# Small query blocks of attention handled for both heads at once, and the head gains loaded and turned earlier, in a decoder trunk on one core

## The chip, the cores and the metric

The kernel runs on one core of a Trainium2 chip. The metric is the device time of one execution in microseconds (us). TensorE is called PE here, VectorE DVE, ScalarE ACT, GpSimd POOL and SyncE SP; PEld is PE's weight load, which runs beside PE's products.

## What is computed

The reference is a causal trunk over 512 tokens of width 1024: one attention layer, one gated short convolution, and a gated MLP with a depthwise convolution behind each. The attention layer is the part that matters here. Its 16 heads of 64 are split into 8 forgetting heads (softmax with a decay added to the logits) and 8 stick-breaking heads. Cut to that:

```
xn = rms_norm(h, norm_g);  proj = xn @ w_in          # q, k, v and 8 forget logits
q_fox, k_fox = rms_norm(q[:8], fox_q_g), rms_norm(k[:8], fox_k_g)
q_sb,  k_sb  = rms_norm(q[8:], sb_q_g),  rms_norm(k[8:], sb_k_g)
# forgetting heads, a block of 128 queries
logits = q @ k.T * scale + cum_f[q] - cum_f[k];  p = softmax(causal(logits));  o = p @ v
# stick-breaking heads
z = q @ k.T * scale;  log_beta = log_sigmoid(z)
log_one_minus = where(strict, log_sigmoid(-z), 0)
later = reverse_cumsum(log_one_minus) - log_one_minus
w = where(strict, exp(log_beta + later), 0);  o = w @ v
h = h + concat(o_fox, o_sb) @ w_out
```

The four head gains (`fox_q_g` and so on) have 64 numbers each.

## The kernel before

Every float32 product is made of three PE products: each operand is split into a high part `hi` (a rounded copy, made by ACT) and the rest `lo` (a subtraction, made by DVE), and `hi*hi`, `lo*hi` and `hi*lo` are added up in one bank of PSUM. The helper lines are L245 to L247 (weights times the normed activations) and L489 to L491 (the value projection). Weight tiles come by SP's queue as `raw` and are split into `whi` (L227) and `wlo` (L228). PSUM is divided into two banks "a" (accumulators), four banks "b" (logits) and two banks "c" (everything that is turned, and small sums).

**Start.** `x` comes in four pieces by SP's queue (L93). PE warms up (L696) and turns `x` into bank tiles (`take`, L717). ACT and DVE split the turned tiles into `hs_hi` and `hs_lo` (`halves_of`, L721 and L722), and PE runs the first projections between the takes. In this stage `in_line` ties each engine's operations into the written order. ACT's queue carries one load here, `first` (L85), ahead of the function table and a warm-up activation. POOL's queue carries the four loads of the head gains (`load_heads`, L90). The gains become a column per head group in `load_head_gains`: a PE transpose of a 4x128 tile (L151), a DVE copy out (L152) and two DVE scalings (L154). That call is put off by the constant `HEADS` of a planner clock, so it comes out behind the second projection. The evictions of the q and k projections (L579, L575 and L576) multiply by these columns.

**Attention.** The heads go in pairs p = 0 to 7 (0 to 3 forgetting, 4 to 7 stick-breaking), each with query blocks b = 0 to 3; block b sees n = 128(b+1) keys. `logits(p, b)` makes the logits of both heads e = 0, 1 in two "b" banks and then the weights `w`. A forgetting head takes a maximum (L611), an exponential with its sum (L613, ACT), a reciprocal (L615) and a product (L616). A stick-breaking head takes two sigmoids (L620 and L621, ACT), a zero in the last column (L623, POOL), a reverse scan (L625) and a product (L626). `turn(p, b)` turns the weights on PE (L645), one "c" bank per head, and splits them into the high `pt` (L648, ACT) and the low `pt` (L649, DVE). `weigh(p, half)` multiplies by the values (L664 and L665) for two blocks together, and its result leaves through L674, L675 and the split at L330 and L331.

**What sets the order.** A planner clock in the Python code (`spend`, `after`, `fill`) deals out the work: between logits, turn and weigh it pulls products from `fillers`, which are generators of q and k projections (`queries_keys`), value projections (`values`) and half of the output projection (`output(0)`). Sums, norms and row scales of the q and k tiles (L525, L533, L561, each in a "c" bank) are put off by constants. A scheduler underneath orders the instructions of each engine again by their dependences and bank releases, so a change in one place can move others.

After the attention (from about 280 us on) come the second half of the output projection, the MLP, the short convolution and the second MLP; the change touches no line of these.

Of the kernel before, what the change touches and what calls it, by code (L numbers as in the profile page):

```python
# [17 lines left out]
F32 = mybir.dt.float32  # L18
F32R = mybir.dt.float32r
BF16 = mybir.dt.bfloat16  # L20
I32 = mybir.dt.int32
AF = mybir.ActivationFunctionType
ALU = mybir.AluOpType
AX = mybir.AxisListType

P = 128
S = 512
NB = S // P
# [4 lines left out]
HD = 64  # L33
# [4 lines left out]
PT = 2  # L38
WB = 4
PRE = 12.0  # L40
SUM_STEP = 0.6
WARM = 34
HEADS, NORM0 = 4.0, 4.6
ORDER = (1, 0, 1, 1, 1, 1, 3)
SUMS, FLAT, ROWS = 3.0, 1.5, 5.0
NSUMS, NROWS = 4.0, 3.0
# [4 lines left out]
def trunk(  # L51
# [6 lines left out]
    nc = tc.nc  # L58
    act, dve, pe, pool = nc.scalar, nc.vector, nc.tensor, nc.gpsimd
# [4 lines left out]
    tiny = ctx.enter_context(tc.tile_pool(name="tiny", bufs=4))  # L64
# [4 lines left out]
    def bank(tag):  # L69
        n_ps[0] += 1  # L70
        return ps.tile([P, S], F32, tag=tag, name=f"ps{tag}{n_ps[0]}", bufs={"a": 2, "b": 4, "c": 2}[tag])

    def f32(ap):
        return ap.bitcast(F32)
# [11 lines left out]
    heads_in = xin.tile([4, P], F32, tag="heads_in", name="heads_in")  # L86

    def load_heads():
        for i, g in enumerate((fox_q_gain, fox_k_gain, sb_q_gain, sb_k_gain)):
            nc.gpsimd.dma_start(heads_in[i:i + 1, :].rearrange("o (j d) -> o j d", j=2), g[:, None, :].to_broadcast([1, 2, HD]))  # L90

    def load_x(q):
        nc.sync.dma_start(x_tok[:, :, q * 256:(q + 1) * 256], xr[:, :, q * 256:(q + 1) * 256])  # L93

    load_x(0)
    warm = tiny.tile([P, 1], F32, tag="warm", name="warm", bufs=1)
    act.activation(warm, blank[:, 0:1], AF.Copy)

# [18 lines left out]
    ident = const.tile([P, P], F32, tag="ident", name="ident")  # L117
    make_identity(nc, ident)

    begin = const.tile([P, S], BF16, tag="begin", name="begin")  # L120
# [28 lines left out]
    def load_head_gains():  # L149
        t = bank("c")  # L150
        pe.transpose(t[:, 0:4], heads_in, ident[0:4, 0:4])  # L151
        dve.tensor_copy(head_gains, t[:, 0:4])  # L152
        for i in (0, 2):
            dve.tensor_scalar(head_gains[:, i:i + 1], head_gains[:, i:i + 1], HD ** -0.5, None, op0=ALU.mult)  # L154
# [29 lines left out]
    def after(us, fn):  # L184
        later.append((clock[0] + us, len(later), fn))
        later.sort(key=lambda e: e[0])
# [312 lines left out]
    halves, q_scale, done = {}, {}, set()  # L499
# [6 lines left out]
    def queries_keys(p):  # L506
# [73 lines left out]
            sqs.append(sq)  # L580
        after(SUMS, sums)

    def logits(p, b):

        fox = p < 4
        need(("qk", p))
        need("decay")
        (k_hi, k_lo), (q_hi, q_lo) = (halves[p][i] for i in range(2))
        n = (b + 1) * P
        wide = max(n, 256)  # L590
        tok = slice(b * P, n)
        ss = [bank("b") for _ in range(2)]
        for step, (ql, kl) in enumerate(((q_hi, k_hi), (q_hi, k_lo), (q_lo, k_hi))):
            for e in range(2):
                rows = slice(e * HD, (e + 1) * HD)
                pe.matmul(ss[e][:, 0:wide], ql[rows, tok], kl[rows, 0:wide], start=step == 0, stop=not fox and step == 2)  # L596
        if fox:
            for e in range(2):
                rows = slice(e * HD, (e + 1) * HD)
                pe.matmul(ss[e][:, 0:wide], dl[rows, p, tok], dr[rows, 0:wide], start=False, stop=False)  # L600
            for e in range(2):
                pe.matmul(ss[e][:, tok], ident16, mask, start=False, stop=True)
        spend((4 if fox else 3) * wide * 0.00044 + (0.12 if fox else 0))
        ws = []
        for e in range(2):
            s = ss[e]
            w = aw.tile([P, S], F32, tag="w", name=f"w{p}{b}{e}", bufs=WB)
            ws.append(w)
            if fox:
                top = tiny.tile([P, 1], F32, tag="top", name=f"top{p}{b}{e}")  # L610
                dve.reduce_max(top, s[:, 0:n], axis=AX.X, negate=True)  # L611
                total = tiny.tile([P, 1], F32, tag="total", name=f"total{p}{b}{e}")
                act.activation(w[:, 0:n], s[:, 0:n], AF.Exp, bias=top, accum_out=total)  # L613
                inv = tiny.tile([P, 1], F32, tag="inv", name=f"inv{p}{b}{e}")
                dve.reciprocal(inv, total)  # L615
                dve.tensor_scalar(w[:, 0:n], w[:, 0:n], inv, None, op0=ALU.mult)  # L616
            else:
                scale = q_scale[p]
                rest = aw.tile([P, S], F32, tag="rest", name=f"rest{p}{b}{e}")
                act.activation(rest[:, 0:n], s[:, 0:n], AF.Sigmoid, scale=scale[:, 1, b, e:e + 1])  # L620
                act.activation(w[:, 0:n - 1], s[:, 0:n - 1], AF.Sigmoid, scale=scale[:, 0, b, e:e + 1])  # L621

                pool.memset(w[:, n - 1:n], 0.0)  # L623
                back = rest[:, 1:n][:, ::-1]
                dve.tensor_tensor_scan(back, back, begin[:, S - n + 1:S][:, ::-1], 0.0, op0=ALU.mult, op1=ALU.max)  # L625
                dve.tensor_tensor(w[:, 0:n - 1], w[:, 0:n - 1], rest[:, 1:n], op=ALU.mult)  # L626
        return ws

    pts = {}

    def turn(p, b, ws):

        half, n = b // 2, (b + 1) * P
        if b % 2 == 0:
            pts[p, half] = []
            for e in range(2):
                both = [aw.tile([P, NB, 256], F32R, tag=f"pt{i}", name=f"pt{p}{half}{e}{i}", bufs=PT) for i in range(2)]
                for t in both:
                    pool.memset(f32(t[:, 2 * half + 1, 0:P]), 0.0)
                pts[p, half].append(both)  # L640
        at_ = slice((b % 2) * P, (b % 2 + 1) * P)
        for e in range(2):
            t = bank("c")
            for k in range(b + 1):
                pe.transpose(t[:, k * P:(k + 1) * P], ws[e][:, k * P:(k + 1) * P], ident)  # L645
            src = t[:, 0:n].rearrange("p (k q) -> p k q", q=P)
            hi, lo = pts[p, half][e]
            act.activation(hi[:, 0:b + 1, at_], src, AF.Copy)  # L648
            dve.tensor_tensor(lo[:, 0:b + 1, at_], src, f32(hi[:, 0:b + 1, at_]), op=ALU.subtract)  # L649
        spend(0.22 * (b + 1))  # L650

    def weigh(p, half):


        need(("v", p // 2))
        v = v_tiles[p // 2]
        acc = bank("a")
        to = slice(half * 256, (half + 1) * 256)
        last = 2 * half + 1
        for e in range(2):  # L660
            hi, lo = pts[p, half][e]
            for k in range(last + 1):
                w = v[:, k, 2 * (p % 2) + e].rearrange("p i d -> p (i d)")
                pe.matmul(acc[:, e * 256:(e + 1) * 256], w, hi[:, k, :], start=k == 0, stop=False)  # L664
                pe.matmul(acc[:, e * 256:(e + 1) * 256], w, lo[:, k, :], start=False, stop=k == last)  # L665
        spend(0.44 * (last + 1))
        if p == 4 and half == 0:
            o_tiles[1] = mixed(1)
        o_hi, o_lo = o_tiles[p // 4]
        total = work.tile([P, S], F32, tag="y", name=f"o{p}{half}")[:, 0:256]  # L670
        for e in range(2):
            own, other = (slice(i * HD, (i + 1) * HD) for i in (e, 1 - e))
            cols = slice(e * 256, (e + 1) * 256)
            act.activation(total[own, :], acc[other, cols], AF.Copy)  # L674
            dve.tensor_tensor(total[own, :], acc[own, cols], total[own, :], op=ALU.add)  # L675
        split(o_hi[:, p % 4, to], o_lo[:, p % 4, to], total)
# [17 lines left out]
    t = bank("c")  # L694
# [4 lines left out]
    t = bank("c")  # L699
# [24 lines left out]
    def keep(f):  # L724
        t = taken.pop(f)
        if f % 2:
            in_line("act", act.activation(h[:, f, :], t, AF.Copy))
        else:
            in_line("dve", dve.tensor_copy(h[:, f, :], t))
# [7 lines left out]
        load_x(q)  # L737
    for i in range(1, 1 + AHEAD):
        ready.append(load(i))
    load_heads()  # L740
    after(HEADS, load_head_gains)
    qk0 = queries_keys(0)
    part, nk = halve.pop(0)

# [15 lines left out]
    for f in range(2, ND):  # L760
        take(f)
        halves_of(f)
        if f == 3:
            keep(0)
            keep(1)
        first_products(ORDER[f - 1])
# [13 lines left out]
    attn = ExitStack()  # L780
    ap_ = attn.enter_context(tc.tile_pool(name="attn", bufs=1))
    aw = attn.enter_context(tc.tile_pool(name="aw", bufs=2))

# [17 lines left out]
    for g in range(len(blocks) + 2):  # L803
# [3 lines left out]
        if g >= 2 and blocks[g - 2][1] % 2:  # L807
            p, b = blocks[g - 2]
# [41 lines left out]
    with tc.tile_pool(name="mlp0", bufs=1) as mp:  # L850
# [3 lines left out]
        for o in range(ND):  # L854
            acc = bank("ab"[o % 2])
            k = 0
            for nk in (8, 7, 7):
                w = weights()
# [7 lines left out]
    with tc.tile_pool(name="mix", bufs=1) as mp:  # L866
# [23 lines left out]
        for o in range(ND):  # L890
            w = weights()
# [7 lines left out]
    with tc.tile_pool(name="mlp1", bufs=1) as mp:  # L899
        a_hi, a_lo = mlp_tiles(mp)  # L900
        up(1, norm, a_hi, a_lo)
        for c in range(2):
# [16 lines left out]
            for k in range(k0):  # L919
                if k % 2 == 0:  # L920
                    w = weights()
# [4 lines left out]
            ws = [weights(AHEAD - i) for i in range(AHEAD + 1)]  # L926
# [31 lines left out]
```

## Time and profile before

| | |
|---|---|
| median of 3 runs | 1225.56 us |
| range of the runs | 1225.53 to 1226.32 us |
| the profiled execution | 1226.17 us |
| its span in the trace | 1224.4 us |
| PE busy | 1207.0 us, 99% of the span |
| DVE busy | 762.8 us, 62% |
| ACT busy | 502.3 us, 41% |

The span is the stretch that the trace covers; 1.77 us of the profiled execution lie around it. Busy time is an average over the whole program, so the stages have to be looked at one by one. A wait that the trace names is an idle stretch of an engine together with what released it. "idle before" in a row is the time in which the engine did nothing just before that instruction.

### The profile page before, as it was taken

To read this page: it belongs to the slowest core of one execution; us is meant where nothing else is said; L and a number is where in the kernel's file an instruction comes from. 1 tells how busy PE (TensorE), PEld (TensorE's weight loads), DVE (VectorE), ACT (ScalarE), POOL (GpSimd) and SP (SyncE) were. 2 spreads that over 40 slices of the span, in tenths; PEclk is the share of its full clock that TensorE was granted. 3 is DMA by queue.
4 is the path that set the end of the run, shared out by engine and by line. 5 is a ranking of instruction groups with operands and counts; after the bars stand their busy time and mean duration, and the time that the engine had idled before them with its cause. 6 is when DMAs were issued, how large, how long until landed. Compare 5 with 4: busy or idle time off the path is not lost.

```text
span 1224.4 us, 15001 instructions
## 1 busy us (share of the span) xinstructions
PE 1207.0 (99%) x5841; PEld 974.7 (80%) x5841; DVE 762.8 (62%) x1249; ACT 502.3 (41%) x787; POOL 26.5 (2%) x139
## 2 busy tenths in 40 slices
PE   8999999999999999999999999999999999999998
PEld 7887877777888888888888888888888888888886
DVE  5887888887767776763333655555776767772222
ACT  6556576555443434342222222233444444342120
POOL 4000000000000000000000000000000000000000
PEclk9999999999999999999999999999999999999999
DMA  7312121212333333333333233333333233322330
GB/s 195 88 36 69 36 69 36 73 56 80 93 97 91 98 90 100 89 91 95 95 95 103 86 92 97 97 93 92 98 86 103 86 104 86 103 86 86 118 106 35
DMA packets 183576, 108.14 MB, mean 88 GB/s; under 512 B 4716, under 2 KB 176796, under 8 KB 183504
## 3 DMA queue, kind: packets, MB, share of 16 engines
q1 hardware_dynamic: 183104, 107.00, 29.6%
q8 instruction: 46, 0.75, 0.3%
q0 software_dynamic: 384, 0.17, 0.1%
q14 instruction: 26, 0.21, 0.1%
q10 hardware_dynamic: 16, 0.00, 0.0%
HBM read 105.06 MB, written 2.10 MB: 88 GB/s over the span
## 4 chain that ended last, share of the span: by engine, by line
PE 90%; DVE 6%; ACT 2%; issue 1%; POOL 0%; DVEq 0%; ACTq 0%
PE psa L245 13%; PE psa L247 13%; PE psa L246 13%; PE psb L245 11%; PE psb L247 11%; PE psb L246 11%; PE psa L489 2%; PE psa L490 2%; PE psa L491 2%; PE psb L490 2%; PE psb L489 2%; PE psb L491 2%; DVE rest L625 1%; PE psc L645 1%; PE psb L596 1%
## 5 line engine op out<-in xcount | busy, mean ns | idle before, releaser
L227 ACT ACTIVATE whi<-raw 128x1024 fp32r<-128x1024 f32 (+3 forms) x199 | 208.6, 1049 | 361.0 <-PE psb L246 131.1
L228 DVE TENSOR_TENSOR wlo<-raw,whi 128x1024 fp32r<-128x1024 f32 (+3 forms) x199 | 240.5, 1209 | 161.0 <-ACT whi L227 160.0
L245 PE MATMUL psa<-hs_hi,whi 128*128 128x512 f32 x544 | 219.4, 403 | 2.3 <-DVE o L675 1.3
L247 PE MATMUL psa<-hs_hi,wlo 128*128 128x512 f32 x544 | 215.1, 395 | 0.3 <-DVE wlo L228 0.2
L246 PE MATMUL psa<-hs_lo,whi 128*128 128x512 f32 x544 | 214.7, 395 | 0.0
L245 PE MATMUL psb<-hs_hi,whi 128*128 128x512 f32 x480 | 189.9, 396 | 0.0
L247 PE MATMUL psb<-hs_hi,wlo 128*128 128x512 f32 x480 | 189.8, 395 | 0.0
L246 PE MATMUL psb<-hs_lo,whi 128*128 128x512 f32 x480 | 188.8, 393 | 0.0
L338 DVE SCALAR_TENSOR_TENSOR u<-y,taps,u 128x510 f32<-128x510 f32 (+1 forms) x176 | 131.1, 748 | 3.0
L245 PEld LDWEIGHTS psa<-hs_hi,whi 128*128 128x128 f32 x544 | 102.3, 188 | 25.6 <-issue 2.3
L247 PEld LDWEIGHTS psa<-hs_hi,wlo 128*128 128x128 f32 x544 | 102.2, 188 | 25.0 <-DVE wlo L228 1.1
L246 PEld LDWEIGHTS psa<-hs_lo,whi 128*128 128x128 f32 x544 | 102.3, 188 | 22.3 <-DVE hs_lo L722 0.4
L246 PEld LDWEIGHTS psb<-hs_lo,whi 128*128 128x128 f32 x480 | 90.1, 188 | 21.4
L247 PEld LDWEIGHTS psb<-hs_hi,wlo 128*128 128x128 f32 x480 | 90.1, 188 | 21.4
L245 PEld LDWEIGHTS psb<-hs_hi,whi 128*128 128x128 f32 x480 | 90.3, 188 | 20.3
L832 DVE TENSOR_TENSOR y<-psb,nrow_n 128x512 f32<-128x512 f32 x44 | 30.4, 692 | 83.9 <-PE psb L247 83.9
L330 ACT ACTIVATE a<-u 128x512 fp32r<-128x512 f32 x44 | 27.9, 634 | 118.6 <-DVE u L837 118.6
L836 ACT ACTIVATE u<-u 128x512 f32<-128x512 f32 x44 | 27.8, 632 | 91.4 <-DVE u L338 91.4
L335 ACT ACTIVATE u<-y,taps 128x512 f32<-128x512 f32 x88 | 63.0, 719 | 0.0
L331 DVE TENSOR_TENSOR a<-u,a 128x512 fp32r<-128x512 f32 x44 | 30.5, 692 | 29.4 <-ACT a L330 29.4
L489 PE MATMUL psa<-whi,hs_hi 128*128 128x256 f32 (+1 forms) x128 | 38.3, 299 | 0.8 <-ACT qk L579 0.7
L491 PE MATMUL psa<-whi,hs_lo 128*128 128x256 f32 (+1 forms) x128 | 36.3, 283 | 0.0
(237 smaller groups left out, 1824.0 us busy)
## 6 DMA issues: line engine op xcount, KB each, us to landing
raw<-in_ffn_w_up SPq DMA_DIRECT2D x88, 512.0 KB, 3.8
raw<-in_ffn_w_down SPq DMA_DIRECT2D x30, 512.0 KB, 3.6
raw<-in_attn_w_in SPq DMA_DIRECT2D x24, 512.0 KB, 4.0
raw<-in_conv_w_in SPq DMA_DIRECT2D x24, 512.0 KB, 3.8
raw<-in_ffn_w_down SPq DMA_DIRECT2D x16, 448.0 KB, 3.6
raw<-in_attn_w_out SPq DMA_DIRECT2D x8, 512.0 KB, 3.4
raw<-in_conv_w_out SPq DMA_DIRECT2D x8, 512.0 KB, 3.8
x_tok<-in_x SPq DMA_DIRECT2D x4, 512.0 KB, 6.8
```

Of the source, the lines that this page charges most:

```text
L227: return (act.activation(hi[:, at_], raw[:, at_], AF.Copy), dve.tensor_tensor(lo[:, at_], raw[:, at_], f32(hi[:, at_]), op=ALU.subtract))
L228: dve.tensor_tensor(lo[:, at_], raw[:, at_], f32(hi[:, at_]), op=ALU.subtract))
L245: made = [pe.matmul(acc, w[0], rhs[0], start=first, stop=False), pe.matmul(acc, w[0], rhs[1], start=False, stop=False), pe.matmul(acc, w[1 ...
L246: pe.matmul(acc, w[0], rhs[1], start=False, stop=False),
L247: pe.matmul(acc, w[1], rhs[0], start=False, stop=last)]
L331: dve.tensor_tensor(lo, src, f32(hi), op=ALU.subtract)
L335: act.activation(dst, src, AF.Copy, scale=tap(2))
L338: dve.scalar_tensor_tensor(dst[:, d:], src[:, 0:S - d], tap(j), dst[:, d:], op0=ALU.mult, op1=ALU.add)
L489: pe.matmul(acc, lhs[0], w[0], start=first, stop=False)
L490: pe.matmul(acc, lhs[0], w[1], start=False, stop=False)
L491: pe.matmul(acc, lhs[1], w[0], start=False, stop=last)
L832: dve.tensor_tensor(y, acc, norm.row, op=ALU.mult)
```

## The change

1. **Head gains.** The four loads of `load_heads` go to ACT's queue, right behind `first`, and so ahead of ACT's table load. `load_head_gains` is no longer put off: it is called after the fourth take in the start, and the constant `HEADS` goes.
2. **Small blocks.** For b < 2 `at_once` gives one slice with both heads, for b of 2 and 3 two slices with one head. Per slice there is one reciprocal (forgetting) or one product (stick-breaking), one "c" bank for the turned weights, one high copy and one low subtraction. With one slice all of it holds both heads: 2 x 128 or 2 x 256 columns.
3. **Zeros.** `rest` becomes one tile that is kept for the whole attention, with a column of zeros at its end, and a stick-breaking block lies at its right end. The product is taken one column further along and meets the zero, so POOL's memset of the last column of `w` goes. The scan and the second sigmoid are one column longer.
4. **Tiles.** `w` is one tile for both heads (two buffers), and `pt` one tile for both heads (one buffer), so its zeros take half as many memsets, each for both heads.

```diff
-HEADS, NORM0 = 4.0, 4.6
+NORM0 = 4.6
...
-            nc.gpsimd.dma_start(heads_in[i:i + 1, :].rearrange("o (j d) -> o j d", j=2), g[:, None, :].to_broadcast([1, 2, HD]))
+            act.dma_start(heads_in[i:i + 1, :].rearrange("o (j d) -> o j d", j=2), g[:, None, :].to_broadcast([1, 2, HD]))
...
     load_x(0)
+    load_heads()
     warm = tiny.tile([P, 1], F32, tag="warm", name="warm", bufs=1)
...
+    def at_once(b):
+        return (slice(0, 2),) if b < 2 else (slice(0, 1), slice(1, 2))
...
+            for es in at_once(b):
+                dve.reciprocal(inv[:, es], total[:, es])
+                for e in range(es.start, es.stop):
+                    dve.tensor_scalar(w[:, e, :], w[:, e, :], inv[:, e:e + 1], None, op0=ALU.mult)
...
+            for es in at_once(b):
+                for e in range(es.start, es.stop):
+                    act.activation(rest[:, e, keys], ss[e][:, 0:n], AF.Sigmoid, scale=scale[:, 1, b, e:e + 1])
+                    act.activation(w[:, e, :], ss[e][:, 0:n], AF.Sigmoid, scale=scale[:, 0, b, e:e + 1])
+                    back = rest[:, e, keys][:, ::-1]
+                    dve.tensor_tensor_scan(back, back, begin[:, keys][:, ::-1], 0.0, op0=ALU.mult, op1=ALU.max)
+                dve.tensor_tensor(w[:, es], w[:, es], rest[:, es, S - n + 1:S + 1], op=ALU.mult)
...
-        for e in range(2):
-            t = bank("c")
-            for k in range(b + 1):
-                pe.transpose(t[:, k * P:(k + 1) * P], ws[e][:, k * P:(k + 1) * P], ident)
...
+        for es in at_once(b):
+            t = bank("c")[:, 0:(es.stop - es.start) * n].rearrange("p (e k q) -> p e k q", k=b + 1, q=P)
+            for e in range(es.start, es.stop):
+                for k in range(b + 1):
+                    pe.transpose(t[:, e - es.start, k, :], w[:, e, k * P:(k + 1) * P], ident)
+            act.activation(hi[:, es], t, AF.Copy)
+            dve.tensor_tensor(lo[:, es], t, f32(hi[:, es]), op=ALU.subtract)
...
-    load_heads()
-    after(HEADS, load_head_gains)
...
         if f == 3:
+            load_head_gains()
             keep(0)
             keep(1)
...
+    rest = aw.tile([P, 2, S + 1], F32, tag="rest", name="rest", bufs=1)
+    pool.memset(rest[:, :, S:S + 1], 0.0)
```

Lines of the changed kernel are shifted by one in most places (its L246 is L245 of before, its L646 is L645). The change moves instructions in three places that matter here.

PE at the start, before: `first` and the first two takes of `x`, then the first projection.

```order
69 L700 MATMUL psc_150<-ident,first 128x8
70 L717 MATMUL psb_174<-ident,x_tok 128x128 x4
71 L717 MATMUL psb_179<-ident,x_tok 128x128 x4
72 L245 MATMUL psa_194<-hs_hi,whi_155 128x512
73 L246 MATMUL psa_194<-hs_lo,whi_155 128x512
```

The same place of the changed kernel.

```order
69 L699 MATMUL psc_154<-ident,first 128x8
70 L716 MATMUL psb_174<-ident,x_tok 128x128 x4
71 L716 MATMUL psb_179<-ident,x_tok 128x128 x4
72 L152 MATMUL psc_212<-ident,heads_in 128x4
73 L246 MATMUL psa_194<-hs_hi,whi_159 128x512
74 L247 MATMUL psa_194<-hs_lo,whi_159 128x512
```

The transpose of the head gains (`heads_in`) now stands ahead of the first projection, and with it PE's wait for the four loads.

PE behind the second projection, before: L151 turns the head gains, L525 makes the sums of squares, L489 to L491 begin the values (`psa_416` is the accumulator of the first group of 24 products).

```order
125 L247 MATMUL psa_280<-hs_hi,wlo_163 128x512
126 L151 MATMUL psc_260<-ident,heads_in 128x4
127 L525 MATMUL psc_451<-sq_276,head_ones 32x128 x4
128 L489 MATMUL psa_416<-whi_166,hs_hi 128x264
129 L490 MATMUL psa_416<-wlo_167,hs_hi 128x264
```

The same place of the changed kernel; `psa_418` is the first group and `psa_446` the second.

```order
126 L248 MATMUL psa_280<-hs_hi,wlo_167 128x512
127 L490 MATMUL psa_418<-whi_170,hs_hi 128x264
128 L491 MATMUL psa_418<-wlo_171,hs_hi 128x264
...
150 L492 MATMUL psa_418<-whi_282,hs_lo 128x264
151 L526 MATMUL psc_453<-sq_276,head_ones 32x128 x4
152 L526 MATMUL psc_453<-sq_399,head_ones 32x128 x3
153 L490 MATMUL psa_446<-whi_170,hs_hi 128x264
```

The values now follow the projection directly, and the sums stand behind their first group.

PE in block b = 1 of pair 3, before: L645 turns the weights of the two heads into two "c" banks (`psc_2091`, `psc_2096`), and L561 turns the row scales of pair 4 into the next one (`psc_2107`).

```order
869 L645 MATMUL psc_2091<-ident,w_1921 128x128 x2
870 L645 MATMUL psc_2096<-ident,w_1929 128x128 x2
871 L489 MATMUL psa_2087<-whi_1607,hs_hi 128x256
...
886 L489 MATMUL psa_2087<-whi_1751,hs_hi 128x256
887 L561 MATMUL psc_2107<-ident,qwide_2005 128x128 x4
888 L490 MATMUL psa_2087<-wlo_1752,hs_hi 128x256
```

The same place of the changed kernel, where L646 is the turn and L562 the row scales.

```order
864 L646 MATMUL psc_1976<-ident,w_1822 128x128 x4
865 L490 MATMUL psa_1972<-whi_1528,hs_hi 128x256
...
870 L492 MATMUL psa_1972<-whi_1528,hs_lo 128x256
871 L562 MATMUL psc_1989<-ident,qwide_1901 128x128 x4
872 L490 MATMUL psa_1972<-whi_1528,hs_hi 128x256
```

Both heads now share one bank, and the row scales stand 6 products behind the turn, where there were 16.

## Rows read from the trace of the kernel before

**Rows 1.** The page, busy time: us (share of the span), instructions.

```profile
PE 1207.0 (99%) x5841; PEld 974.7 (80%) x5841; DVE 762.8 (62%) x1249; ACT 502.3 (41%) x787; POOL 26.5 (2%) x139
```

**Rows 2.** Windows: length, busy PE, PEld, DVE, ACT, POOL, PE clock, DMA share, GB/s.

```profile
7.00:22.00 15.00, 14.71 (x72) 11.03 (x72) 11.05 (x15) 12.86 (x22) 5.96 (x16) 1.00 0.69 191
50.00:280.00 230.00, 219.66 (x1466) 175.24 (x1465) 186.76 (x465) 140.70 (x321) 13.71 (x92) 0.99 0.19 54
267.00:276.00 9.00, 7.02 (x35) 5.68 (x34) 6.55 (x12) 3.97 (x8) 0.00 (x0) 0.81 0.14 40
280.00:1224.40 944.40, 940.53 (x4081) 760.27 (x4079) 541.91 (x698) 331.58 (x419) 0.00 (x0) 1.00 0.31 93
```

**Rows 3.** Waits of PE, 50 to 280 us: total, times, longest.

```profile
PE psc L645 <- DVE pt L649: 3.6, 4, 1.4
...
PE psc L561 <- DVE pt L649: 1.4, 2, 0.9
...
PE psc L561 <- DVE qwide L554: 0.5, 1, 0.5
```

**Rows 4.** Timeline of PE behind the second projection: start, duration, instruction.

```profile
22.13 0.22 PE L151 MATMUL psc<-ident,heads_in 4*128 4x4 f32 x1
22.86 0.42 PE L525 MATMUL psc<-sq,head_ones 128*32 128x128 f32 x8 [0.51 <-DVE head_gains L152]
23.71 0.39 PE L489 MATMUL psa<-whi,hs_hi 128*128 128x264 f32 x1 [0.42 <-ACT qk L579]
...
27.55 0.43 PE L525 MATMUL psc<-sq,head_ones 128*32 128x128 f32 x8
27.90 0.39 PE L489 MATMUL psa<-whi,hs_hi 128*128 128x264 f32 x1
```

**Rows 5.** Timeline of ACT there.

```profile
24.49 0.72 ACT L579 ACTIVATE qk<-psa,head_gains 128x512 f32<-128x512 f32 x1
```

**Rows 6.** Timeline of PE at the start.

```profile
4.91 1.10 PE L717 MATMUL psb<-ident,x_tok 128*128 128x128 f32 x8
6.99 0.50 PE L245 MATMUL psa<-hs_hi,whi 128*128 128x512 f32 x1 [0.99 <-ACT whi L227]
```

**Rows 7.** Timeline of ACT at the start.

```profile
0.73 0.62 ACTq L85 DMA_DIRECT2D first<-in_attn_norm  x1
...
5.60 0.69 ACT L721 ACTIVATE hs_hi<-psb,first_gains 128x512 fp32r<-128x512 f32 x1 [2.73 <-PE psb L717]
```

**Rows 8.** Timeline of SP's queue at the start.

```profile
1.76 2.67 SPq L93 DMA_DIRECT2D x_tok<-in_x  x3
```

**Rows 9.** DMA queues, 0 to 3.2 us: ACT's queue, which carries `first` alone.

```profile
q10 hardware_dynamic: 16, 0.00, 0.6%
```

**Rows 10.** Line L90, the four loads of the head gains on POOL.

```profile
DMA to landing us min/median/max: 5.0/5.6/5.8
```

**Rows 11.** Timeline of PE in block 1 of pair 3.

```profile
143.40 0.60 PE L645 MATMUL psc<-ident,w 128*128 128x128 f32 x4
...
146.80 0.66 PE L561 MATMUL psc<-ident,qwide 128*128 128x128 f32 x4 [0.92 <-DVE pt L649]
```

**Rows 12.** Timeline of DVE there.

```profile
143.60 0.42 DVE L554 COPY qwide<-qr 128x512 f32<-128x512 f32 x1
...
146.33 0.75 DVE L649 TENSOR_TENSOR pt<-psc,pt 128x256 fp32r<-128x256 f32 x2
```

**Rows 13.** Timeline of PE in block 1 of pair 7.

```profile
256.05 0.47 PE L245 MATMUL psa<-o_hi,whi 128*128 128x512 f32 x1 [0.27 <-DVE o L675]
```

**Rows 14.** DVE groups by shape, 50 to 280 us: busy, mean ns, idle before.

```profile
L615 DVE RECIPROCAL inv<-total 128x1 f32<-128x1 f32 x32 | 5.0, 159 | 2.4 <-ACT w L613 2.4
...
L649 DVE TENSOR_TENSOR pt<-psc,pt 128x128 fp32r<-128x128 f32 x16 | 4.4, 288 | 3.7 <-ACT pt L648 1.6 <-POOL pt L639 1.3 <-POOL w L623 0.8
```

**Rows 15.** Timeline of DVE and PE in block 0 of pair 0, all engines.

```profile
54.00 0.28 DVE L616 TENSOR_SCALAR w<-w,inv 128x128 f32<-128x128 f32 x1
...
55.41 0.27 PE L645 MATMUL psc<-ident,w 128*128 128x128 f32 x1
```

More of the change, by code (lines that the diff above doesn't have):

```diff
@@ L603, in logits @@
         spend((4 if fox else 3) * wide * 0.00044 + (0.12 if fox else 0))
-        ws = []
-        for e in range(2):
[L606 to L626, printed above, removed]
@@ L627, in logits @@
-        return ws
+        w = aw.tile([P, 2, S], F32, tag="w", name=f"w{p}{b}", bufs=2)[:, :, 0:n]
+        if fox:
+            top, total, inv = (tiny.tile([P, 2], F32, tag=t, name=f"{t}{p}{b}") for t in ("top", "total", "inv"))
+            for e in range(2):
+                dve.reduce_max(top[:, e:e + 1], ss[e][:, 0:n], axis=AX.X, negate=True)
+                act.activation(w[:, e, :], ss[e][:, 0:n], AF.Exp, bias=top[:, e:e + 1], accum_out=total[:, e:e + 1])
+            for es in at_once(b):
+                dve.reciprocal(inv[:, es], total[:, es])
+                for e in range(es.start, es.stop):
+                    dve.tensor_scalar(w[:, e, :], w[:, e, :], inv[:, e:e + 1], None, op0=ALU.mult)
+        else:
+            scale = q_scale[p]
+            keys = slice(S - n, S)
+            for es in at_once(b):
[5 more added lines that the diff above has]
+                dve.tensor_tensor(w[:, es], w[:, es], rest[:, es, S - n + 1:S + 1], op=ALU.mult)
@@ L629, in trunk, with turn @@
+        return w
     pts = {}
-    def turn(p, b, ws):
+    def turn(p, b, w):
         half, n = b // 2, (b + 1) * P
         if b % 2 == 0:
[L635 to L642, printed above, removed]
-            t = bank("c")
-            for k in range(b + 1):
-                pe.transpose(t[:, k * P:(k + 1) * P], ws[e][:, k * P:(k + 1) * P], ident)
[L646 to L649, printed above, removed]
+            pts[p, half] = [aw.tile([P, 2, NB, 256], F32R, tag=f"pt{i}", name=f"pt{p}{half}{i}", bufs=1) for i in range(2)]
+            for t in pts[p, half]:
+                pool.memset(f32(t[:, :, 2 * half + 1, 0:P]), 0.0)
+        hi, lo = (t[:, :, 0:b + 1, (b % 2) * P:(b % 2 + 1) * P] for t in pts[p, half])
+        for es in at_once(b):
[5 more added lines that the diff above has]
+            dve.tensor_tensor(lo[:, es], t, f32(hi[:, es]), op=ALU.subtract)
@@ L660, in weigh @@
         for e in range(2):
-            hi, lo = pts[p, half][e]
+            hi, lo = (t[:, e] for t in pts[p, half])
             for k in range(last + 1):
```

## The prediction

> **What bounds the kernel now.** I began with the page: PE is busy for 1207.0 of the span's 1224.4 us [rows 1], so all that a change can remove is PE's idle time or work on PE, and this change leaves PE's products as they are. The windows show where the 17.4 idle us lie [rows 2]. From 280 us to the end PE stands still for 944.40 - 940.53 = 3.9 us, in code that is not touched. From 50 to 280 us, the attention, it is 230.00 - 219.66 = 10.3 us, and DVE is busy for 186.76 of those 230 us (81%). From 7 to 22 us it is only 0.3 us: what delays PE there is not caught up again. Third, the waits: in the attention PE mostly waits for DVE [rows 3], above all for the low half `pt`, which gives back a "c" bank. Fourth, the timelines, wait by wait.
>
> The sum is made against the profiled execution, 1226.17 us, whose span is 1224.4 with 1.77 us around it. It lies 0.61 us above the median of 1225.56, so a saving of s is forecast as 1225.56 - s. No change means within 0.2%, that is 2.45 us, about what a measurement of this kernel can tell.
>
> **Head gains, where they stood.** PE begins L151 at 22.13 us and the values at 23.71 us [rows 4]. In these 1.58 us it turns the gains, waits 0.51 us for DVE's copy of them and 0.42 us for ACT's L579, which needs the same gains to clear an accumulator, and makes four of the eight sums of squares. The later set of four costs 27.90 - 27.55 = 0.35 us where nothing is waited for [rows 4]. In the new order the values follow the projection at once and the sums stand behind their first group, so they are still paid: 1.58 - 0.35 = **1.2 us saved**. The next limit is ACT's second L579, which frees the accumulator of the second group at 24.49 + 0.72 = 25.2 us [rows 5]. The new order only moves operations on ACT ahead of it that were ahead before, so it ends there still, while 24 products of the first group and seven sums keep PE to about 25.4 us (estimate: the 31 value products between the two L525 rows take 27.55 - 23.71 = 3.84 us, 0.12 each, so 22.1 + 24 x 0.12 + 0.4). That is late enough by 0.2 us only, hence the bounds: 0 (ACT's chain moves along) to 1.6 (the sums cost nothing).
>
> **Head gains, where they go.** This adds one wait: PE's transpose stands behind the first two takes and ahead of the first projection, and PE runs its queue in order. PE is free there from 4.91 + 1.10 = 6.0 us and begins the projection at 6.99 us, since it waits for ACT [rows 6]. So loads that have landed by 6.9 us cost nothing. On ACT, `first` took 0.62 us to issue, and ACT stood idle for 2.73 us before its first real operation at 5.60 us [rows 7]; four issues at 0.62 are 2.48 us and fit in by 0.25 us. SP's issues under load took 2.67 / 3 = 0.89 us [rows 8]; at that price ACT would be 0.8 us late. When the loads land is not shown for this queue: `first`, issued at 0.73, was through by 3.2 us [rows 9], 2.5 us; on POOL the same loads took 5.0 to 5.8 us [rows 10]. By the first, the last load (issued from 1.35 + 3 x 0.62 = 3.2 us) lands at 5.7 us, by the second at 9.0 us, 2.0 us too late, which row by row of 7 to 22 us nothing would win back. I take the first, since it is the queue that they will use, and cost the wait at **nothing**; bounds 0 and +2.8 (0.89 an issue, then 5.8 us: 4.0 + 5.8 = 9.8). SP's later loads now wait for semaphores that the head loads use too; this is covered as long as the heads land in time. POOL loses four issues and its memsets, and nothing on the path waits for POOL.
>
> The Trainium skill (DMA: Bandwidth & Descriptors, section on queues, rings and completion order) says that a DMA engine serves the queues it has work for in turn, a packet at a time. By that the heads would pass the backlog of `x` as `first` did, 0 us lost. The same page (latency and other measured facts) gives 0.2 us for an access to HBM, but 2 us under high load, and `first` went out while the engines were still empty; an estimate with 1.8 us more is 7.5 us, 0.5 us lost. No row here decides between the two.
>
> **Small blocks.** Sixteen blocks (b of 0 and 1, eight pairs) lose one ACT copy and one DVE subtraction each, eight lose a reciprocal of 159 ns and eight a product. Two subtractions of 128 columns at 288 ns each [rows 14] become one of 256; the steps overlap in part, so I put DVE's relief at 0.2 us a block (estimate; at the least 0, at the most the removed subtraction's 0.29 and a reciprocal's 0.16), 3 us over the attention, 1.6% of its busy time there. DVE is not PE's bound throughout, so only what it shortens in front of a wait of PE counts:
>
> - Pair 3, block 1. L561 wants the next "c" bank and waits 0.92 us for the low half of the first head, which DVE reaches only at 146.33 us behind the weights of block 2 [rows 11, 12]. In the new order both heads share one bank, so L561 takes the other, which was free long before, and its input is ready at 143.60 + 0.42 = 144.0 us [rows 12]. **0.9 us saved** (bounds 0 and 0.92).
> - Pair 7, block 1. PE waits 0.27 us for an eviction of `o` at 256.05 us [rows 13]; now the four transposes of this block are put ahead of it and fill the gap. **0.3 us** (0 to 0.5).
> - Pair 0, block 1: L561 waits 0.5 us for `qwide` [rows 3], since a subtraction goes between; it is now two products later. **0.2 us** (0 to 0.5).
> - The longest waits, L645 for `pt` (3.6 us over four) [rows 3], belong to blocks 2 and 3, which keep their form: **nothing** (0 to 1.0, should DVE come to them earlier).
>
> Joint weights could make PE wait for the second head. In the first block, the tightest that I found, the second weights end at 54.00 + 0.28 = 54.28 us and the first transpose starts at 55.41 us [rows 15]: 1.1 us of room. Nothing is lost.
>
> **Sum**: 1.2 + 0.9 + 0.3 + 0.2 = 2.6 us. Against the profiled execution 1223.6 us, against the median **1222.9 us**.
>
> **Rivals.**
> - *Late heads.* The loads share the DMA engines with `x` and land at 9.8 us, as on POOL; PE stands from 6.0 to 9.8 us. Price: 2.8 - 1.2 = +1.6 us. After PE's idle time around 268 us the granted clock in 267 to 276 us was 0.81, part of it at 1.2 instead of 2.4 GHz [rows 2]; the like of it here costs 0.19 x 9 = 1.7 us more. With 1.4 us won in the attention: 1225.56 + 1.6 + 1.7 - 1.4 = **1227.5**, slower than before. It decides from a landing at 6.9 us on. For it: POOL's 5.0 to 5.8 us. Against: `first`.
> - *The attention gives nothing.* PE arrives earlier at the next wait for DVE in block 2 or 3 and waits longer there. Only the start is won: **1224.4**, no change. For it: those waits are the longest.
> - *DVE's relief carries on.* DVE comes up to 1.0 us sooner to blocks 2 and 3, and the shorter wait there spares part of the slow stretch behind 268 us: 1222.9 - 1.0 - 0.9 = **1221.0**.
> - *The start gives nothing*, because ACT, and not the gains, sets when the second value group starts: 1225.56 - 1.4 = **1224.2**.
>
> **How the numbers follow.** Forecast 0.42 (three quarters of it below 1223.1), late heads 0.20 (half of it above 1228.0, half within), nothing in the attention 0.18, relief carries 0.12, nothing at the start 0.08. Faster by over 0.2%: 0.32 + 0.12 = 0.44. Slower by over 0.2%: 0.10, with 0.01 for what I have not seen. Same: 0.45. The forecast's own range is 1221.8 to 1224.0. The whole range goes from 1220.8 (relief carries) to 1226.8 (late heads without all of the slow clock).
>
> **What would show it.** Right: PE's first projection still at about 7.0 us, behind the gains' transpose; no idle time between projection and values at 22 us, and the second value group some 1.2 us sooner; the 0.92 us before pair 3's L561 gone; the waits of L645 for `pt` in blocks 2 and 3 as before. Wrong: PE idle until 8 us or more at the start, released by a load; a lower clock in the first 22 us; or PE's waits for DVE between 50 and 280 us adding up as before at other lines.

## The result

The changed kernel takes 1229.36 us (median of 10 runs, 1226.13 to 1230.15) against 1225.99 us before (10 runs); the ratio is 1.0025, 95% interval 1.0015 to 1.0035. It is slower, by about 3 us (3.4 between the medians), where 2.6 us less was forecast. The page and the windows of the changed kernel answer to [rows 1, 2]:

```profile
span 1227.4 us, 14829 instructions
...
PE 1208.4 (98%) x5841; PEld 977.2 (80%) x5841; DVE 760.6 (62%) x1217; ACT 500.9 (41%) x771; POOL 18.7 (2%) x72
```

The windows (length, busy PE, PEld, DVE, ACT, POOL, PE clock, DMA share, GB/s):

```profile
0.00:22.00 22.00, 17.05 (x96) 14.20 (x97) 9.68 (x17) 11.31 (x18) 5.99 (x35) 0.84 0.72 193
6.00:9.70 3.70, 0.07 (x1) 0.10 (x1) 2.70 (x4) 1.89 (x4) 0.55 (x3) 0.76 0.96 229
9.70:14.70 5.00, 5.00 (x18) 4.19 (x19) 1.86 (x6) 1.86 (x3) 0.00 (x0) 0.50 1.13 327
14.70:22.00 7.30, 7.09 (x37) 5.38 (x36) 4.85 (x7) 5.56 (x9) 0.30 (x1) 1.00 0.30 80
50.00:280.00 230.00, 220.13 (x1469) 176.05 (x1467) 186.71 (x438) 139.10 (x304) 8.80 (x30) 0.99 0.20 56
270.00:279.00 9.00, 6.96 (x35) 5.65 (x34) 6.49 (x12) 3.69 (x7) 0.00 (x0) 0.81 0.17 47
```

The loss is in the start: PE does next to nothing from 6 to 9.7 us, and then works for 5.0 us at half the clock (0.50, the level of 1.2 GHz), until 14.7 us. The clock behind 268 us falls as before, 3 us later, with the same 0.81. The timeline of PE at the start, for [rows 6], names the wait:

```profile
4.79 1.09 PE L716 MATMUL psb<-ident,x_tok 128*128 128x128 f32 x8
9.63 0.24 PE L152 MATMUL psc<-ident,heads_in 4*128 4x4 f32 x1 [3.75 <-DMA heads_in<-in_sb_k_gain]
9.80 0.80 PE L246 MATMUL psa<-hs_hi,whi 128*128 128x512 f32 x1
10.39 0.63 PE L247 MATMUL psa<-hs_lo,whi 128*128 128x512 f32 x1
```

The gains' transpose waits for the last head load, and the first projection, for which ACT was done by about 7.2 us, stands behind it. L246 takes 0.80 us here and 0.50 us before [rows 6]: the clock. ACT's queue issued the loads in good time, as [rows 7] let one expect:

```profile
1.39 0.71 ACTq L90 DMA_DIRECT2D heads_in<-in_fox_q_gain  x1
...
3.32 0.56 ACTq L90 DMA_DIRECT2D heads_in<-in_sb_k_gain  x1
3.91 1.28 ACT L98 ACT_TABLE_LOAD   x1 [3.91 <-issue]
5.21 0.20 ACT L98 ACTIVATE warm<-blank 128x1 f32<-128x1 bf16 x1
5.48 0.69 ACT L720 ACTIVATE hs_hi<-psb,first_gains 128x512 fp32r<-128x512 f32 x1
```

So the last load let PE go at about 9.6 us, 6.3 us after its issue began at 3.32. To see where the time goes and comes back, the starts of the same PE instructions are read from the four traces that matter (us; in brackets the distance to before; the last two columns are experiments that follow; a row named after logits is the start of the logits of that query block):

| PE starts | before | changed | small blocks alone | gains on POOL, turned in between |
|---|---|---|---|---|
| first projection | 6.99 | 9.79 (+2.80) | 7.34 (+0.35) | 7.08 (+0.08) |
| last product of the last take of x | 13.58 | 18.20 (+4.62) | 13.88 (+0.30) | 14.22 (+0.64) |
| third value group | 30.42 | 34.03 (+3.61) | 30.74 (+0.32) | 30.05 (-0.37) |
| logits of pair 3, block 2 | 141.27 | 144.58 (+3.31) | 141.23 (-0.04) | 140.53 (-0.74) |
| logits of pair 4 | 153.81 | 156.06 (+2.25) | 152.71 (-1.09) | 152.00 (-1.81) |
| logits of pair 7, block 2 | 254.98 | 257.24 (+2.25) | 253.90 (-1.08) | 253.12 (-1.87) |
| logits of pair 7, block 3 | 262.92 | 265.65 (+2.73) | 262.32 (-0.60) | 261.56 (-1.36) |
| last product of weights and values | 275.12 | 277.93 (+2.81) | 273.04 (-2.08) | 272.29 (-2.83) |
| last product of the kernel | 1220.13 | 1222.93 (+2.80) | 1218.04 (-2.09) | 1217.28 (-2.85) |

The changed kernel loses 4.6 us by the last take, wins 1.0 us back at the values and 1.4 us in the attention (1.1 of it between the logits of pair 3, block 2, and those of pair 4), and loses 0.6 us again at its end, 0.5 of it in pair 7 between the logits of blocks 2 and 3.

### The profile page after: what moved, and what is told of

Same layout as the page of the kernel before. It is cut to its first block, busy times and chain, and to the rows that moved or that the text cites. A ratio compares the mean times of both kernels' runs of the same rounds, so it can differ in the third digit from the quotient of the medians.

```text
span 1227.4 us, 14829 instructions
## 1 busy us (share of the span) xinstructions
PE 1208.4 (98%) x5841; PEld 977.2 (80%) x5841; DVE 760.6 (62%) x1217; ACT 500.9 (41%) x771; POOL 18.7 (2%) x72
## 4 chain that ended last, share of the span: by engine, by line
PE 91%; DVE 6%; ACT 2%; issue 1%; DMA 1%; ACTq 0%; DVEq 0%
PE psa L246 13%; PE psa L248 13%; PE psa L247 13%; PE psb L246 11%; PE psb L248 11%; PE psb L247 11%; PE psa L490 3%; PE psa L491 3%; PE psa L492 3%; PE psb L491 2%; PE psb L490 2%; PE psb L492 2%; DVE rest L628 1%; PE psb L601 1%; PE psc L646 1%
## 5 line engine op out<-in xcount | busy, mean ns | idle before, releaser
L246 PE MATMUL psa<-hs_hi,whi 128*128 128x512 f32 x544 | 220.0, 404 | 1.2 <-DVE o L674 1.2
L246 PE MATMUL psb<-hs_hi,whi 128*128 128x512 f32 x480 | 189.9, 396 | 0.0
L246 PEld LDWEIGHTS psa<-hs_hi,whi 128*128 128x128 f32 x544 | 102.5, 188 | 24.3 <-issue 2.3
L246 PEld LDWEIGHTS psb<-hs_hi,whi 128*128 128x128 f32 x480 | 90.3, 188 | 20.3
```

The source lines that it names most:

```text
L246: made = [pe.matmul(acc, w[0], rhs[0], start=first, stop=False), pe.matmul(acc, w[0], rhs[1], start=False, stop=False), pe.matmul(acc, w[1 ...
```

## The experiments

Two theories stood at first. **S**: the start alone loses, the small blocks win. **J**: joining the heads costs by itself. For the late loads there were two more. **F**: the load of `f_bias`, which is POOL's first transfer now that the head loads are gone from there, collides with them. **Q**: the loads are late because of their place in time, behind `x`. F came from the DMA view, 6 to 8.5 us, of the changed kernel:

```profile
DMA packets 441, 0.41 MB, mean 162 GB/s; under 512 B 44, under 2 KB 441, under 8 KB 441
...
q1 hardware_dynamic: 408, 0.40, 58.0%
q0 software_dynamic: 27, 0.00, 34.2%
```

and the same view of the kernel before:

```profile
DMA packets 975, 0.89 MB, mean 357 GB/s; under 512 B 105, under 2 KB 975, under 8 KB 975
...
q1 hardware_dynamic: 897, 0.89, 107.9%
q0 software_dynamic: 78, 0.00, 2.0%
```

POOL's queue (q0) has only 27 packets, of `f_bias`, but they take 34% of the DMA engines' time, and all queues together move less than half as much. Before, POOL issued `f_bias` at 5.02 us, behind the head loads; now at 2.58 us. In the kernel before, `f_bias` lands at 11.4 us, 6.4 us after its issue; from 8.5 to 10.6 us POOL's queue takes 5.4% there, and all queues move 327 GB/s.

**The small blocks alone.** The start of before with the attention of the changed kernel:

```diff
-            act.dma_start(heads_in[i:i + 1, :]...
+            nc.gpsimd.dma_start(heads_in[i:i + 1, :]...
...
-    load_heads()
     warm = tiny.tile(...)
...
+    load_heads()
+    after(HEADS, load_head_gains)
     qk0 = queries_keys(0)
```

> The small blocks as changed, the head gains loaded on POOL and turned behind the second projection as before. Theory S (the start alone loses: the changed kernel's first projection begins at 9.79 us instead of 6.99, and at the lower clock; its attention gained): the start is as before (first projection near 7.0 us), PE reaches the logits of pair 4 some 1.0 to 1.4 us sooner than before against the same starting point, total 0.4 to 1.4 us below the kernel before. Rival J (joining the heads itself costs, by longer waits of PE for DVE): total 1 us or more above the kernel before.

Measured: 1224.35 us, ratio 0.9992 (0.9983 to 1.0001), 1.1 us under the 1225.42 us of its kernel before; the interval just reaches no change, but not the 1 us more that J asked for. S holds and J falls: PE gains 1.4 us between the third value group and pair 4 (+0.32 to -1.09 in the table). 1.1 us of that comes in pair 3 behind the logits of block 2 (-0.04 to -1.09), where the turn of block 1 stands, in place of [rows 11]:

```profile
143.36 0.60 PE L645 MATMUL psc<-ident,w 128*128 128x128 f32 x4
...
144.51 0.60 PE L561 MATMUL psc<-ident,qwide 128*128 128x128 f32 x4
```

The wait of 0.92 us before L561 is gone, as the order promised. The waits of PE between 50 and 280 us, for [rows 3], show what stayed:

```profile
PE psc L645 <- DVE pt L647: 3.9, 4, 1.5
PE psa L245 <- DVE h L689: 1.8, 2, 1.2
PE psa L245 <- DVE o L673: 1.8, 2, 1.3
PE psc L561 <- DVE qwide L554: 0.6, 2, 0.4
...
PE psc L561 <- DVE pt L647: 0.4, 1, 0.4
```

The four long waits of L645 in blocks 2 and 3 are still there (3.9 us in place of 3.6), and so is that for `qwide`; L561's wait for `pt` fell from 1.4 to 0.4 us. In pair 7, 0.5 us is lost (-1.08 to -0.60), and there the new order costs. The four transposes of block 1 now stand ahead of the product that waited 0.27 us for `o` [rows 13]. But that product now waits 0.58 us for `h`, which gives back an accumulator. The changed kernel has the same wait; its PE and DVE there:

```profile
259.19 0.50 PE L246 MATMUL psa<-o_hi,whi 128*128 128x512 f32 x1 [0.57 <-DVE h L690]
...
257.19 0.69 DVE L629 TENSOR_TENSOR w<-w,rest 128x512 f32<-128x512 f32 x1
257.80 0.41 DVE L674 TENSOR_TENSOR o<-psa,o 64x256 f32<-64x256 f32 x1
258.13 0.41 DVE L648 TENSOR_TENSOR pt<-psc,pt 128x256 fp32r<-128x256 f32 x1
258.46 0.67 DVE L690 TENSOR_TENSOR h<-psa,h 128x512 f32<-128x512 f32 x1
```

DVE comes to `h` behind the joint product and the joint subtraction. All eight kernels with the small blocks joined have this wait, of 0.56 to 0.58 us; the two with the attention of before have 0.26 or 0.27 us, for `o`. Whether DVE is late there by the joining or by PE's earlier arrival, no run separates.

The further 1.5 us in the last rows of the table is the clock: in this profile it stayed at its upper level behind 268 us,

```profile
267.00:276.00 9.00, 6.47 (x38) 5.03 (x37) 7.09 (x14) 4.16 (x9) 0.00 (x0) 1.00 0.20 59
```

where before it was 0.81 [rows 2], though the waits of 1.46 and 0.48 us in that place are as in the changed kernel. Whether it falls differs from execution to execution of the same kernel (of the 33 runs of the kernel before, 12 have a mean clock of 0.998 and 21 of 0.999 or 1.000), so this 1.5 us is not put down to the change. Between runs at 0.999 or more the small blocks gain 0.8 us (medians 1225.05 before and 1224.29).

**The start alone.** The changed start with the attention of before (`load_heads` on ACT's queue and `load_head_gains` in the start, nothing else).

> The head gains as changed (ACT's queue, turned ahead of the first projection), the small blocks as before. Theory S: the start loses as in the changed kernel (first projection 9.2 to 9.9 us, values near 26.7 us), nothing is gained in the attention up to pair 4; total 1229 to 1231.5, 3.5 to 5.5 us above the kernel before. If the two parts hide each other (rival): not above the changed kernel's 1229.4 by more than 0.3 us.

Measured: 1229.7 us (4 runs), ratio 1.0037 (1.0024 to 1.0051), 4.0 us above its kernel before. The first projection began at 10.12 us, 0.2 us later than expected, the values at 26.31:

```profile
9.99 0.19 PE L152 MATMUL psc<-ident,heads_in 4*128 4x4 f32 x1 [4.51 <-DMA heads_in<-in_sb_k_gain]
```

S holds; within the intervals the two parts add up (+4.0 here and -1.1 with the small blocks alone make +2.9; measured together +3.4).

**The gains turned later.** The loads stay on ACT's queue, the transpose is tied in line ahead of the fifth take:

```diff
-        pe.transpose(t[:, 0:4], heads_in, ident[0:4, 0:4])
+        in_line("pe", pe.transpose(t[:, 0:4], heads_in, ident[0:4, 0:4]))
...
     for f in range(2, ND):
+        if f == 4:
+            load_head_gains()
         take(f)
...
         if f == 3:
-            load_head_gains()
             keep(0)
```

> The changed kernel with the transpose of the head gains tied in line ahead of the fifth take of x (about 10 us), so that the first projection does not stand behind it. Theory F (the loads are late because f_bias, now POOL's first transfer, runs at 6 to 8 us with 256-byte packets of 0.3 to 1.8 us and slows every load, the second piece of x too): the first projection is back at about 7.0 us, but the third take still waits for x until 10 us, 2 us later than before; total 1224.5 to 1227.5. Theory Q (only the small loads on ACT's queue are late, behind the backlog of x): the third take is at 8.2 us again and the total 2 to 3 us below the kernel before.

Measured: 1226.02 us, ratio 1.0006 (0.9997 to 1.0015). Its timeline of PE:

```profile
6.99 0.50 PE L246 MATMUL psa<-hs_hi,whi 128*128 128x512 f32 x1 [1.31 <-ACT whi L228]
...
9.21 1.09 PE L716 MATMUL psb<-ident,x_tok 128*128 128x128 f32 x8 [0.99 <-DMA x_tok<-in_x]
...
10.93 0.22 PE L152 MATMUL psc<-ident,heads_in 4*128 4x4 f32 x1
...
12.76 0.66 PE L716 MATMUL psc<-ident,x_tok 128*128 128x128 f32 x4 [0.31 <-DVE head_gains L153]
```

The first projection is back at 6.99 us, in this profile with no lower clock (1.00 from 6 to 13 us), and of the 3.4 us above the kernel before 0.6 are left (its kernel before took 1225.42): PE's place behind the loads made most of the loss. The runs spread from 1224.58 to 1228.21 us, and the four above 1227 have a mean clock of 0.997 or less. The third take still waits 0.99 us for `x` and comes 1.0 us later than before, not 2: F in kind, half its size.

**`f_bias` held back.** The changed kernel with that load tied behind POOL's first other small load, so that it goes out at 22.1 us:

```diff
-        q.dma_start(f_bias, attn_f_bias.to_broadcast([P, 8]))
-        q.dma_start(small[0:16, :], ffn_norm...
+        made = q.dma_start(small[0:16, :], ffn_norm...
...
+        behind(q.dma_start(f_bias, attn_f_bias.to_broadcast([P, 8])), made)
         for layer in range(2):
```

> The changed kernel with the load of f_bias put behind POOL's other small loads (near 22 us); the head gains still turned ahead of the first projection. Theory F: no slow packets before 10 us, the head loads land by 7 to 7.7 us, the first projection begins by 7.0 to 7.9 us at full clock; total 1.5 to 3 us below the kernel before. Theory Q: the head loads still land at 9 us or later, PE waits as in the changed kernel, total about 1229.

Measured: 1227.64 us, ratio 1.0016 (1.0007 to 1.0025), between the two forecasts.

```profile
9.01 0.19 PE L152 MATMUL psc<-ident,heads_in 4*128 4x4 f32 x1 [2.33 <-DMA heads_in<-in_sb_k_gain]
9.14 0.50 PE L246 MATMUL psa<-hs_hi,whi 128*128 128x512 f32 x1
```

Its windows:

```profile
6.00:9.70 3.70, 1.37 (x8) 1.07 (x7) 2.83 (x6) 2.40 (x4) 0.00 (x0) 1.00 1.09 357
9.70:13.00 3.30, 3.30 (x13) 2.77 (x12) 0.99 (x2) 1.65 (x3) 0.00 (x0) 0.51 1.13 320
```

The DMA engines move 357 GB/s again from 6 to 9.7 us (229 in the changed kernel), but the last head load still releases PE only at 9.0 us. So `f_bias` accounts for some 0.65 us of the first projection's 2.8 us (9.79 to 9.14; one trace each, and the start alone, with the same loads as the changed kernel, had 10.12); the other 2.15 us are left to Q. The clock fell here too, to 0.51 between 9.7 and 13 us.

**Both.** `f_bias` held back and the gains turned ahead of the fifth take (the two diffs above together).

> Both: f_bias held back and the head gains turned ahead of the fifth take. Under theory F and theory Q alike the first projection begins at about 7.0 us and the third take at 8.2 us, no lower clock in the first 22 us, the values begin 1.2 to 1.6 us sooner than before (near 22.2 us), total 1223 to 1223.8, 2 to 3 us below the kernel before. Theory J: above 1225.

Measured: 1224.51 us, ratio 0.9992 (0.9983 to 1.0001), 0.9 us under its kernel before.

```profile
8.84 1.09 PE L716 MATMUL psb<-ident,x_tok 128*128 128x128 f32 x8 [0.28 <-DMA x_tok<-in_x]
```

The third take came at 8.84 us with a wait of 0.28 us for `x`, against 0.99 us with `f_bias` early: 0.7 us, which is what F is worth in waiting. Between the medians it is 1.5 us (1226.02 to 1224.51), of which 0.9 us remains between runs with a mean clock of 0.999 or more. The total missed the forecast by 0.7 us: the values began only at 23.49 us, since the last take is still 1.5 us late (15.03), by the wait for `x`, the transpose and 0.32 us in which the sixth take waits for DVE's copy of the gains out of its bank.

**The head loads ahead of `first`.** On ACT's queue, with the changed kernel otherwise:

```diff
-    act.dma_start(first, attn_norm[0]...
...
     load_heads()
+    act.dma_start(first, attn_norm[0]...
```

> The changed kernel with the four head loads ahead of first on ACT's queue. Theory Q (a small load is late when it is issued after the DMA engines have filled with x, whatever its shape): the first two head loads, issued by 1.4 us, land by 3.5 us as first did, and first, now issued after 3 us, lands at 5.5 us or later, so PE's transpose of first and the takes begin late, and the total is above 1229. Rival (the shape of the head loads, 2 x 64 numbers on one partition, makes them slow): first still lands near 3 us after its issue, at 5 to 6 us, and the heads land at 8 us or later whatever their place.

One run: 1230.34 us. `first`, issued at 3.77 us in place of 0.73, let PE go only at 9.7 us:

```profile
9.71 0.24 PE L699 MATMUL psc<-ident,first 8*128 8x8 f32 x1 [4.91 <-DMA first<-in_attn_norm]
```

That is 5.9 us after its issue, where `first` in its old place was through 2.5 us after it [rows 9]. The same load with the same shape is late when it is issued late, as Q has it; but here it stands behind the four head loads on ACT's queue as well as behind `x`, and this run does not tell the two apart. The other half of the forecast failed: the head loads, now foremost, were not through by 3.5 us. ACT's queue (q10) shows no packet up to 3.2 us and 4 up to 5 us. In the trace's DMA records the data packets of 256 bytes, which are the head loads' own, start from 3.67 to 8.50 us, and from 5.22 to 9.00 us in the changed kernel: issued 0.65 us sooner at the first and 0.15 us at the last, they are still late. So the shape is not cleared.

**The gains on POOL again, turned ahead of the fifth take.** The small blocks, `load_heads` where it stood before, and the in-line transpose of above.

> The small blocks as changed; the head gains loaded on POOL as before (landing up to 9.9 us) but turned in line ahead of the fifth take of x, where PE arrives near 9.8 us. If the loss of the change is the place of the loads on ACT's queue and of their transpose alone, the first projection is at 7.0 us and the third take at 8.2 us again, the fifth take at most 0.5 us late (the gains' transpose, and the copy of its bank ahead of the sixth take), the values begin 1.2 to 1.7 us sooner against the last take than before, and the total is 2 to 3 us below the kernel before. If the turning in the start costs by itself (rival), the last take is 1 us or more late and the total is no better than with the small blocks alone (1224.35).

Measured: 1225.14 us, ratio 0.9993 (0.9984 to 1.0002): no better than the small blocks alone, as the rival said. The last take is 1.3 us late (14.88): 0.30 us of waiting for `x` at the third take, the transpose, and 0.31 us in which the sixth take waits for DVE's copy.

**The same, with the copy earlier.** DVE's copy goes ahead of its split of the fourth take:

```diff
+        if f == 3:
+            first_products(ORDER[f - 1])
+            load_head_gains()
+            halves_of(f)
+            keep(0)
+            keep(1)
+            continue
         halves_of(f)
```

> As the run before, but DVE's copy of the turned gains is put ahead of its split of the fourth take, so that the bank is free before the sixth take. PE's wait of 0.3 us for that copy, seen where the gains were turned ahead of the fifth take, goes; total 0.2 to 0.4 us below that of the run before. Rival: DVE waits for the late loads itself and delays the split, then no better.

Measured: **1223.69 us**, ratio 0.9988 (0.9979 to 0.9997), 2.0 us under its kernel before and 1.5 us under the run above: more than forecast, because the clock stayed up more often: 7 of its 11 runs had a mean clock of 0.999 or more, 5 of 11 in the run above. Of those runs alone the medians are 1223.59 and 1223.97 us, 0.4 us apart, as forecast. This version beats both kernels, the one before by 0.4 to 2.6 us (the interval).

```profile
9.62 0.40 PE L247 MATMUL psa<-hs_hi,wlo 128*128 128x512 f32 x1
10.31 0.19 PE L151 MATMUL psc<-ident,heads_in 4*128 4x4 f32 x1 [0.30 <-DMA heads_in<-in_sb_k_gain]
10.44 0.66 PE L715 MATMUL psc<-ident,x_tok 128*128 128x128 f32 x4
...
11.63 0.60 PE L715 MATMUL psc<-ident,x_tok 128*128 128x128 f32 x4
```

The sixth take (11.63) no longer waits; what is left is 0.30 us for the last head load. Its window behind 22 us shows PE without a gap, 28.00 of 28.00 us, where the kernel before had 27.07:

```profile
22.00:50.00 28.00, 28.00 (x188) 24.48 (x187) 22.94 (x69) 15.40 (x27) 0.52 (x1) 1.00 0.50 133
```

## Why the prediction was wrong

- **The step that failed** is the one on the loads' landing: "I take the first, since it is the queue that they will use, and cost the wait at nothing". Between the 2.5 us of `first` [rows 9] and POOL's 5.0 to 5.8 us [rows 10], the nearest row was not that of the same queue but that of the same time. `first` went out at 0.73 us, together with the first piece of `x`; the head loads, like POOL's, went out behind it, and the last took 6.3 us until PE could go on. Whether their place in time alone made them late, or their shape too, the run with the heads ahead of `first` leaves open. The prediction's rival *Late heads* is what happened: it put the landing at 9.8 us, and PE was let go at 9.6. The price of its wait was right (2.8 us); the clock's price was put at 1.7 us and came to 1.8 us (+2.80 at the first projection, +4.62 at the last take; PE does not pause between the two, so that all of it is the lower clock). Term by term the rival had +2.8 for the wait, -1.2 at the values, +1.7 for the clock and -1.4 in the attention, together +1.9; the trace has +2.80, -1.0, +1.8, -1.4 and +0.6 at the end of the attention, together +2.8. By the prediction's own numbers this case had 0.20, and the range ended at 1226.8, below even the 1227.5 of this very rival; both were set too low. The clock's part differs from run to run: of the ten runs of the changed kernel seven have a mean clock of 0.995 (1228.84 to 1230.15 us), and the fastest has 0.998 (1226.13 us).
- **What stood in front was not costed.** The prediction listed that POOL loses four issues and said that nothing on the path waits for POOL. But a queue that loses work also issues its next transfer sooner: `f_bias` moved from 5.02 to 2.58 us and took a third of the DMA engines' time at the moment in which `x` and the gains had to land. The two pairs of runs on it give it 0.65 and 0.7 us of PE's waiting; in the medians, with what the clock adds, it is 1.2 us (3.4 us above the kernel before to 2.2) and 1.5 us.
- **The Trainium skill** (DMA: Bandwidth & Descriptors, section on queues, rings and completion order) lets a DMA engine serve its queues in turn, a packet at a time; by that the heads should have passed the backlog of `x`. The trace does not show them passing it: the views of ACT's queue up to 5 us and from 5 to 9.7 us of the changed kernel both read the same,

```profile
q10 hardware_dynamic: 16, 0.00, 0.3%
```

so in the first 5 us only the 16 packets of `first` moved, though the four head loads were issued by 3.9 us. The 2 us that the same page's section on latency allows for an access under load made 7.5 us, which was nearer and still 2 us short. Whether the loads wait in the engines or before them is not settled by these runs.
- **Head gains, where they stood**: right in kind, 1.2 us forecast, 1.0 measured (+4.62 at the last take to +3.61 at the third value group; the same 1.0 in the kernel with both repairs, +1.46 to +0.44).
- **SP's later loads**, which the prediction let wait for the heads' semaphores: no cost in the start. Behind the gains' transpose PE waits for a weight tile once up to 22 us, for 0.21 us, as before.
- **Pair 3, block 1**: right; 0.9 forecast, 1.1 measured.
- **Pair 0, block 1**: 0.2 us forecast, nothing measured. The waits for `qwide` are still 0.5 to 0.6 us in all.
- **Pair 7, block 1**: 0.3 us of gain forecast, 0.5 us of loss measured (+2.25 at the logits of block 2 to +2.73 at those of block 3). The transposes did move ahead of the waiting product, but its wait went over from `o` to `h` and grew from 0.27 to 0.57 us. The prediction looked for such a cost of joint weights in the first block alone, and put it at nothing.
- **The waits in blocks 2 and 3**: no shorter, as said (3.6 us before, 3.9 now). DVE's relief did not carry on to them, though it is about as large as estimated: the low copies of the small blocks took 6.3 + 4.4 us before and take 5.5 (eight of 685 ns) + 3.3 now, the reciprocals 5.0 and now 2.4 + 1.3, 3.2 us together (on the page DVE's busy time fell by 2.2 us, from 762.8 to 760.6). The first row is of the kernel before, beside [rows 14], the others of the changed one:

```profile
L649 DVE TENSOR_TENSOR pt<-psc,pt 128x256 fp32r<-128x256 f32 x16 | 6.3, 416 | 0.9 <-ACT pt L648 0.8
...
L648 DVE TENSOR_TENSOR pt<-psc,pt 128x512 fp32r<-128x512 f32 x24 | 16.2, 685 | 2.5 <-ACT pt L647 2.3
...
L648 DVE TENSOR_TENSOR pt<-psc,pt 128x256 fp32r<-128x256 f32 x8 | 3.3, 419 | 2.9 <-ACT pt L647 2.8
L616 DVE RECIPROCAL inv<-total 128x1 f32<-128x1 f32 x16 | 2.4, 158 | 1.1 <-ACT w L614 1.0
...
L616 DVE RECIPROCAL inv<-total 128x2 f32<-128x2 f32 x8 | 1.3, 164 | 3.2 <-ACT w L614 3.2
```

## What to carry to other kernels

When a load moves to another queue, take its landing from a load that was issued at the same time under the same traffic, not from one of the same queue at another time; and where an in-order engine is put behind that load, the price is the whole wait and what the lower clock behind it costs. Look also at what the old queue now issues sooner. Merging small operations pays only in front of a wait: 2 to 3 us of DVE's time went, and PE gained 1.1 us at one place and lost 0.5 us at another, where the freed wait only moved to the next thing that DVE had to deliver.

## What the runs showed of the hardware

- After 3.75 us without work PE's granted clock was 0.50 for the next 5.0 us (9.7 to 14.7); after 2.33 us (with `f_bias` held) the first projection still ran at the upper level (L246 took 0.50 us) and the clock was 0.51 from 9.7 to 13 us; with idle times of 1.31 us at the first projection and 0.99 us at the third take (gains turned later) it stayed at 1.00.
- Behind 268 us the same two waits (1.46 and 0.48 us) were followed by a lower clock in the changed kernel and by none in the kernel with the small blocks alone. The stretch from the logits of pair 7, block 2, to the last product of weights and values took 20.69 us with it (257.24 to 277.93) and 19.14 us without (253.90 to 273.04).
- 4 KB for `f_bias`, read as one row for 128 partitions, took 34% of the time of all DMA engines between 6 and 8.5 us and what they moved was 162 GB/s, against 357 before and 361 with the load held back; before, issued 2.4 us later, the same load went by almost unseen (327 GB/s from 8.5 to 10.6 us). Why is open.
